# The diagonal of the HGRN2 scores from eight 64-by-64 products instead of four 128-by-128 ones

## The chip, the cores and the metric

The kernel runs on one core of a Trainium2 chip, in one launch. The metric is the device time of one execution in microseconds (us), the median of three runs: 2370.31 us before the change (2369.54 to 2370.97). All numbers by engine come from one profiled execution of the kernel before.

Five engines take part. PE (TensorE) multiplies matrices and writes the results to PSUM; PEld is its weight load. DVE (VectorE) and ACT (ScalarE) do elementwise work and read PSUM. POOL (GpSimd) does elementwise work too. SP (SyncE) issues the transfers (DMA). Each engine works through its own list of instructions in order, and waits where an instruction needs what another engine has not yet finished.

## The reference

Two layers over x of shape [1, 2048, 1024], in float32. Each layer scales and shifts x by a vector made from c, runs mixers over it, projects the result and adds it to x under a layer norm. Layer 0 holds two mixers, an HGRN2 mixer of four heads of 128 channels and an RWKV7 mixer of eight heads of 64; layer 1 is an RG-LRU. The change lies in the HGRN2 mixer, of which this is the core:

```python
log_f = log(lb + (1 - lb) * sigmoid(z));  k = (1 - lb) * sigmoid(-z)
b = cumsum(log_f) within a chunk of 64 steps
# inside a chunk, for t >= s:
s[t, s] = sum_k q[t, k] * k[s, k] * exp(b[t, k] - b[s, k])
o = s @ i + (q * exp(b)) @ S_in            # S_in: the state carried from chunk to chunk
S_out = exp(b_last) * S_in + (k * exp(b_last - b))^T @ i
o = o * rsqrt(mean(o * o) + eps) * norm_g
```

For t = s the decay factor is exp(0) = 1, so the diagonal of the scores is only the sum over k of q[t, k] * k[t, k].

## The kernel before, in words

The 2048 steps are worked through in two halves (superblocks, `sb`) of 1024, and each of these in two blocks (`b`) of 512. Channels lie on the 128 partitions and time on the free axis. For layer 0, `mix0` (L1227) writes PE's order out by hand: a generator of projections (x times the weights; lines L431 to L433, three products for each pair of tiles) is stepped, and between its steps the steps of the other tasks are put in when they come due: `rate_steps`, `b_steps` (RWKV7) and `a_steps` (HGRN2), for four groups `g` and two blocks `b` each. So PE's list interleaves projections with short pieces of both mixers. The order on DVE and ACT is chosen by the scheduler.

`a_steps` (L630) runs 16 times: 4 heads, 2 superblocks, 2 blocks. Here a run of it is called by the time at which its diagonal products start, as "the run at 202". It builds the score matrix of a block in one standing tile `st` [128, 512], four 128-by-128 squares of two chunks each, as `st[s, t]`:

- Six levels of distance h = 32, 16, 8, 4, 2, 1. For a level, `decays` (L656) makes the decay-weighted k and q (L664 to L667 on DVE, an exponential on ACT), and `scores` (L670) multiplies them: PE, line L679, 64-row by 32-column products for each half square. The result in PSUM (`sc`) is copied to `st` under a mask of the level (L694 on DVE, `copy_predicated`; level 32 by ACT, L691).
- The diagonal: four products of 128 by 128 (L711), `kf` (k) against `q`, into a PSUM tile `scd`; then one masked copy of 128x512 (L712) with `dmask`, the identity.
- The products between the two chunks of a square (`s6`, L730), and the state.

`scd` lies in the PSUM buffer with tag "ta", which the neighbouring steps of `a_steps` use as well. Right behind the diagonal, PE's list has, in 12 of the 16 runs, the first half of the RWKV7 score products of the next block (`psc`, L905), then projections, the state products `pn` (L1078, L1087), and the second half of `psc`. The `psc` tiles share the two "tb" buffers: the second half can only start when DVE has read the first half out of them (L912). The two runs for g = 3 of each superblock have no `psc` behind them; in these, and in the state chain of RWKV7 generally, PE's L1087 and DVE's L1090 take turns: each state product needs the state that DVE has just scaled.

Where the two engines meet (L711 and L712 are changed, the rest is not):

```python
pscs = [ps.tile([P, 4, P], F32, name=f"psc_{nm}_{hd}_{c4}", tag="tb", bufs=2) for hd in range(2)]   # L900
nc.vector.tensor_mul(sc[:, hd, c4 * 4 : c4 * 4 + 4], pscs[hd], msk)                                # L912
```

Of the kernel before, what the change touches and what calls it, by code (L numbers as in the profile page):

```python
# [13 lines left out]
F32 = mybir.dt.float32  # L14
# [9 lines left out]
P = 128  # L24
D = 1024
KT = 8
BLK = 512
# [41 lines left out]
def tile_encoder(  # L69
# [19 lines left out]
    nc = tc.nc  # L89
# [28 lines left out]
    ps = ctx.enter_context(tc.tile_pool(name="ps", bufs=1, space=PSUM))  # L118
# [174 lines left out]
    dmask = cst.tile([P, P], U8, name="dmask")  # L293
# [332 lines left out]
    for i in range(1):  # L626
        t = cst.tile([P, BLK], F32, name=f"st_{i}")
        nc.gpsimd.memset(t, 0.0)
        st_tiles.append(t)
    def a_steps(hh, sb, b, us):  # L630

        q, z, iv = (us[i][b][:, 0:BLK] for i in range(3))
        nm = f"a{hh}_{sb}_{b}"

        def t2k(tag, bufs=1, dt=F32):
            return tp.tile([P, BLK], dt, name=f"{tag}_{nm}", tag=tag, bufs=bufs)
# [11 lines left out]
        kf = t2k("a_e")  # L648
# [3 lines left out]
        st = st_tiles[0]  # L652
# [3 lines left out]
        def decays(li):  # L656

            h = LEVELS[li]
            w = tp.tile([P, BLK], F32, name=f"w{li}_{nm}", tag="a_w", bufs=2)
            if h == 1:  # L660
                nc.scalar.activation(w, lf, AF.Exp)
            else:
                mid = half(bb, h)[:, :, 0, h - 1 : h].broadcast_to([P, BLK // (2 * h), h])
                nc.vector.tensor_add(half(w, h)[:, :, 0], half(kz, h)[:, :, 0], mid)  # L664
                nc.vector.tensor_sub(half(w, h)[:, :, 1], half(bb, h)[:, :, 1], mid)
                nc.scalar.activation(w, w, AF.Exp)
            nc.vector.tensor_mul(half(w, h)[:, :, 1], half(w, h)[:, :, 1], half(q, h)[:, :, 1])  # L667
            return kf if h == 1 else w, w

        def scores(lis, ws):  # L670

            sc = ps.tile([P, 2, 4, 32], F32, name=f"sc{lis[0]}_{nm}", tag="oa")
            for i, (li, (left, right)) in enumerate(zip(lis, ws)):
                h = LEVELS[li]
                m = 32 if h == 32 else 64
                for j in range(4):
                    for hf in range(2):
                        o_ = j * P + 64 * hf
                        nc.tensor.matmul(  # L679
                            sc[64 * hf : 64 * hf + m, i, j], left[:, o_ : o_ + m],  # L680
                            half(right[:, o_ : o_ + 64], h)[:, :, 1], start=True, stop=True,
                        )
            for i, li in enumerate(lis):
                h = LEVELS[li]
                m = 32 if h == 32 else 64
                for hf in range(2):
                    rows = slice(64 * hf, 64 * hf + m)
                    stv = st.rearrange("p (j b n two h) -> p j b n two h", j=4, b=2, two=2, h=h)[rows, :, hf, :, 1]
                    scv = sc[rows, i].rearrange("p j (n h) -> p j n h", h=h)
                    if h == 32:  # L690
                        nc.scalar.copy(stv, scv)  # L691
                    else:
                        mask = lmask[rows, li].rearrange("p (j n h) -> p j n h", j=1, h=h)
                        nc.vector.copy_predicated(stv, mask.broadcast_to([m, 4, 32 // h, h]), scv)  # L694
# [10 lines left out]
        ws = decays(1), decays(2)  # L705
        yield 4
        scores((1, 2), ws)
        sc = ps.tile([P, BLK], F32, name=f"scd_{nm}", tag="ta")
        for j in range(4):
            js = slice(j * P, (j + 1) * P)  # L710
            nc.tensor.matmul(sc[:, js], kf[:, js], q[:, js], start=True, stop=True)  # L711
        nc.vector.copy_predicated(  # L712
            st.rearrange("p (j t) -> p j t", j=4), dmask.rearrange("p (j t) -> p j t", j=1).broadcast_to([P, 4, P]),
            sc.rearrange("p (j t) -> p j t", j=4),
        )
        ws = decays(3), decays(4)

        v64 = lambda t: t.rearrange("p (c t) -> p c t", t=64)
# [29 lines left out]
        for j in range(4):  # L748
            js = slice(j * P, (j + 1) * P)
# [20 lines left out]
        for j in range(4):  # L770
            js = slice(j * P, (j + 1) * P)
# [26 lines left out]
    for i in range(2):  # L798
        t = cst.tile([P, 8, 64], F32, name=f"tt_{i}")
# [427 lines left out]
    def mix0(sb, hs, w_first):  # L1227
# [30 lines left out]
        for g in range(4):  # L1258
            for b in range(2):
                early = 4 if g == 3 and b else 0  # L1260
                tasks.append((34 + 48 * g + 24 * b - early, rate_steps(g, sb, b, lr, sgi_of)))
                tasks.append((40 + 48 * g + 24 * b - early, (g, b, b_steps, ub)))
                tasks.append((64 + 48 * g + 24 * b, (g, b, a_steps, ua)))
# [136 lines left out]
```

## Time and profile before

| what | value |
|---|---|
| median of three runs | 2370.31 us (2369.54 to 2370.97) |
| profiled execution, its own time | 2367.25 us, span 2365.5 us |
| PE busy | 2194.7 us, 93% of the span |
| PEld busy | 1727.5 us, 73% |
| DVE busy | 1455.6 us, 62% |
| ACT busy | 1264.6 us, 53% |
| POOL busy | 557.7 us, 24% |
| mean granted clock of PE | 0.969 of full speed |

How to read it: an engine's busy time is the time in which it executes something; the rest is waiting. PE is busy nearly all the time, so a place at which PE waits for another engine is rare, and each can be looked up. The page's table of 40 slices shows that PE's clock (PEclk) is at full speed in most slices. A float32 product shows as two records in the trace, so four products of L711 are eight records. In a timeline, equal instructions behind one another are merged ("x8"), and the idle time before an instruction stands in brackets with what ended it. A start minus the start before it is the pace at which the engine goes through its list; durations of neighbours overlap a little.

### The profile page before, as it was taken

Reading aid. Unit: us, or ns where it says so; the run is one execution under the profiler, and the core shown is the slowest. Engines: PE = TensorE matmul, PEld = TensorE weight load, DVE = VectorE, ACT = ScalarE, POOL = GpSimd, SP = SyncE. Lnnn points to the kernel's source line nnn. Section 1 sums busy time; section 2 is a strip of 40 time slices with the busy share of each in tenths; the row PEclk is TensorE's granted clock in tenths of the full one; section 3 lists DMA queues with packets and bytes.
Section 4 is the critical chain, followed back from the end, with each engine's and each line's share of the span. In section 5 each row is a group of like instructions: output and inputs, shape, how many; then the busy total and the mean of one; then the engine's idle time right before and its main releaser. Section 6 shows DMA issues by size and latency. Waiting matters only on the chain. (4 is left out here: it accounts for less than half of the span.)

```text
span 2365.5 us, 45520 instructions
## 1 busy us (share of the span) xinstructions
PE 2194.7 (93%) x18400; PEld 1727.5 (73%) x18400; DVE 1455.6 (62%) x2697; ACT 1264.6 (53%) x2035; POOL 557.7 (24%) x586
## 2 busy tenths in 40 slices
PE   5989999999999999799999999899999999989998
PEld 4767777777777877577677777678777788767776
DVE  6546666667643678466675666436766556766366
ACT  4344655446666633445565456774467643666541
POOL 3311111212111322112111111112334331353321
PEclk7989999999999999899999999999999999999999
DMA  8210111111332637111111113326311564112652
GB/s 299 92 38 27 40 36 35 44 25 42 97 114 82 223 123 248 35 31 38 33 41 35 44 25 118 112 84 237 130 59 63 169 218 156 63 58 94 200 182 98
DMA packets 185938, 229.82 MB, mean 97 GB/s; under 512 B 65912, under 2 KB 99320, under 8 KB 185728
## 3 DMA queue, kind: packets, MB, share of 16 engines
q1 hardware_dynamic: 185728, 226.92, 30.1%
q8 instruction: 144, 2.36, 0.4%
q14 instruction: 66, 0.54, 0.1%
HBM read 175.46 MB, written 51.39 MB: 96 GB/s over the span
## 5 line engine op out<-in xcount | busy, mean ns | idle before, releaser
L431 PE MATMUL pp_g<-hl_h,wh_g 128*128 128x512 f32 x512 | 212.0, 414 | 4.0 <-ACT go L595 4.0
L433 PE MATMUL pp_g<-hh_h,wl_g 128*128 128x512 f32 x512 | 204.0, 398 | 4.0 <-POOL wl_g L368 4.0
L432 PE MATMUL pp_g<-hh_h,wh_g 128*128 128x512 f32 x512 | 204.4, 399 | 0.0
L368 POOL TENSOR_TENSOR wl_g<-raw_g,wh_g 128x512 fp32r<-128x512 f32 x64 | 97.5, 1528 | 349.9 <-ACT wh_g L367 307.8
L431 PE MATMUL po<-hl_wo,wh_mx 128*128 128x512 f32 x448 | 176.3, 393 | 4.0 <-DVE y L527 4.0
L433 PE MATMUL po<-hh_wo,wl_mx 128*128 128x512 f32 x448 | 175.4, 391 | 0.0
L432 PE MATMUL po<-hh_wo,wh_mx 128*128 128x512 f32 x448 | 174.9, 390 | 0.0
L431 PE MATMUL pp_b<-hl_h,wh_b 128*128 128x512 f32 x384 | 167.8, 437 | 5.1 <-ACT cr_b L838 5.1
L431 PE MATMUL pp_a<-hl_h,wh_a 128*128 128x512 f32 x384 | 168.9, 440 | 0.0
L432 PE MATMUL pp_b<-hh_h,wh_b 128*128 128x512 f32 x384 | 153.5, 400 | 0.0
L432 PE MATMUL pp_a<-hh_h,wh_a 128*128 128x512 f32 x384 | 153.4, 399 | 0.0
L433 PE MATMUL pp_a<-hh_h,wl_a 128*128 128x512 f32 x384 | 153.1, 399 | 0.0
L433 PE MATMUL pp_b<-hh_h,wl_b 128*128 128x512 f32 x384 | 152.7, 398 | 0.0
L368 POOL TENSOR_TENSOR wl_a<-raw_a,wh_a 128x512 fp32r<-128x512 f32 x48 | 66.9, 1402 | 329.0 <-ACT wh_a L367 329.0
L368 POOL TENSOR_TENSOR wl_mx<-raw_mx,wh_mx 128x512 fp32r<-128x512 f32 x64 | 80.8, 1268 | 255.7 <-ACT wh_mx L367 255.7
L368 POOL TENSOR_TENSOR wl_b<-raw_b,wh_b 128x512 fp32r<-128x512 f32 x48 | 67.4, 1409 | 269.1 <-ACT wh_b L367 260.0
L431 PEld LDWEIGHTS pp_g<-hl_h,wh_g 128*128 128x128 f32 x512 | 99.0, 193 | 27.8 <-ACT go L595 4.9
L433 PEld LDWEIGHTS pp_g<-hh_h,wl_g 128*128 128x128 f32 x512 | 99.0, 193 | 27.6 <-POOL wl_g L368 5.7
L587 DVE TENSOR_TENSOR go<-go,oi 128x512 f32<-128x512 f32 x64 | 45.9, 722 | 111.0 <-DMA oi<-o_dr 63.8
L432 PEld LDWEIGHTS pp_g<-hh_h,wh_g 128*128 128x128 f32 x512 | 99.4, 194 | 18.9
L433 PE MATMUL pp_c<-hh_h,wl_c 128*128 128x512 f32 x256 | 101.3, 397 | 11.0 <-POOL wl_c L368 9.6
L431 PE MATMUL pp_c<-hl_h,wh_c 128*128 128x512 f32 x256 | 101.6, 397 | 2.7 <-DVE hl_h L368 2.6
(355 smaller groups left out, 5677.8 us busy)
## 6 DMA issues: line engine op xcount, KB each, us to landing
adw<-in_ada_w_dram SPq DMA_DIRECT2D x96, 256.0 KB
oi<-o_dr SPq DMA_DIRECT2D x64, 256.0 KB
m_dr<-go SPq DMA_DIRECT2D x56, 256.0 KB
raw_b<-in_w_ev_dram SPq DMA_DIRECT2D x48, 256.0 KB
raw_a<-in_w_ev_dram SPq DMA_DIRECT2D x48, 256.0 KB
raw_g<-in_w_ev_dram SPq DMA_DIRECT2D x32, 256.0 KB
wo<-in_w_evo_dram SPq DMA_DIRECT2D x32, 256.0 KB
raw_mx<-m_dr SPq DMA_DIRECT2D x32, 256.0 KB
```

The source lines that it names most:

```text
L368: return (eng or nc.vector).tensor_tensor(out=lo, in0=src, in1=hi.bitcast(F32), op=ALU.subtract)
L431: nc.tensor.matmul(pt, ah, bl, start=first, stop=False)
L432: nc.tensor.matmul(pt, ah, bh, start=False, stop=False)
L433: nc.tensor.matmul(pt, al, bh, start=False, stop=last)
L587: nc.vector.tensor_mul(go[b], go[b], oi[b])
```

## The change

The four 128-by-128 products of the diagonal become eight of 64 by 64, one for each chunk: for `hf` = 0 they write PSUM partitions 0 to 63, for `hf` = 1 partitions 64 to 127, in turn, as the level scores of L679 do. All 128 channels are still summed over. The PSUM tile shrinks to [128, 4, 64]. Since the two halves now lie at other places of `st`, the one masked copy of 128x512 becomes two of 64x256, one for each half.

```diff
-        sc = ps.tile([P, BLK], F32, name=f"scd_{nm}", tag="ta")
+        sc = ps.tile([P, 4, 64], F32, name=f"scd_{nm}", tag="ta")
         for j in range(4):
-            js = slice(j * P, (j + 1) * P)
-            nc.tensor.matmul(sc[:, js], kf[:, js], q[:, js], start=True, stop=True)
-        nc.vector.copy_predicated(
-            st.rearrange("p (j t) -> p j t", j=4), dmask.rearrange("p (j t) -> p j t", j=1).broadcast_to([P, 4, P]),
-            sc.rearrange("p (j t) -> p j t", j=4),
-        )
+            for hf in range(2):
+                o_ = slice(j * P + 64 * hf, j * P + 64 * hf + 64)
+                nc.tensor.matmul(sc[64 * hf : 64 * hf + 64, j], kf[:, o_], q[:, o_], start=True, stop=True)
+        for hf in range(2):
+            rows = slice(64 * hf, 64 * hf + 64)
+            mask = dmask[rows, 64 * hf : 64 * hf + 64].rearrange("p (j t) -> p j t", j=1)
+            nc.vector.copy_predicated(
+                st.rearrange("p (j b t) -> p j b t", b=2, t=64)[rows, :, hf], mask.broadcast_to([64, 4, 64]), sc[rows]
+            )
```

Line numbers behind the diagonal grow by three (L905 becomes L908, L912 L915, L1090 L1093). PE's list is otherwise the same. The scheduler moves a few instructions on DVE.

DVE at the diagonal of the first run, before. L694 copies the level scores, L664 and L665 prepare the next two levels, L667 finishes them:

```order
L694 COPY_PREDICATED st_348<-lmask,sc_a_0_0_1706 64x4x4x8 x2
L664 TENSOR_TENSOR w_a_0_0_1733<-a_kz_a_0_0_1448,a_b_a_0_0_1446 128x64x4
L712 COPY_PREDICATED st_348<-dmask,scd_a_0_0_1727 128x512
L665 TENSOR_TENSOR w_a_0_0_1733<-a_b_a_0_0_1446 128x64x4
L664 TENSOR_TENSOR w_a_0_0_1738<-a_kz_a_0_0_1448,a_b_a_0_0_1446 128x128x2
```

The same place of DVE's list, after:

```order
L694 COPY_PREDICATED st_348<-lmask,sc_a_0_0_1706 64x4x4x8 x2
L716 COPY_PREDICATED st_348<-dmask,scd_a_0_0_1727 64x4x64 x2
L664 TENSOR_TENSOR w_a_0_0_1738<-a_kz_a_0_0_1448,a_b_a_0_0_1446 128x64x4
L665 TENSOR_TENSOR w_a_0_0_1738<-a_b_a_0_0_1446 128x64x4
L664 TENSOR_TENSOR w_a_0_0_1743<-a_kz_a_0_0_1448,a_b_a_0_0_1446 128x128x2
```

The masked copies now stand ahead of the first L664; everything from the second L664 on follows in the same order as before, down to L912. It is the same in the other runs with a `psc` behind them.

DVE at the diagonal of the last run of the first superblock (g = 3, b = 1), before. L1090 scales the state that PE's next L1087 needs; L587 belongs to the output gate:

```order
L664 TENSOR_TENSOR w_a_0_1_7712<-a_kz_a_0_1_7463,a_b_a_0_1_7461 128x128x2
L712 COPY_PREDICATED st_348<-dmask,scd_a_0_1_7701 128x512
L587 TENSOR_TENSOR go_0_4_7537<-go_0_4_7537,oi_1_0_0_7668 128x512
L665 TENSOR_TENSOR w_a_0_1_7712<-a_b_a_0_1_7461 128x128x2
L720 TENSOR_TENSOR a_kz_a_0_1_7463<-a_kz_a_0_1_7463,a_b_a_0_1_7461 128x512
L1090 TENSOR_SCALAR sb_b_0_1_7628<-pn_b_0_1_7629,lam_b_0_1_6516 128x64
L667 TENSOR_TENSOR w_a_0_1_7707<-w_a_0_1_7707,u_a_3_1_6542 128x64x4
```

The same place, after:

```order
L716 COPY_PREDICATED st_348<-dmask,scd_a_0_1_7736 64x4x64 x2
L587 TENSOR_TENSOR go_0_4_7572<-go_0_4_7572,oi_1_0_0_7703 128x512
L664 TENSOR_TENSOR w_a_0_1_7752<-a_kz_a_0_1_7498,a_b_a_0_1_7496 128x128x2
L665 TENSOR_TENSOR w_a_0_1_7752<-a_b_a_0_1_7496 128x128x2
L723 TENSOR_TENSOR a_kz_a_0_1_7498<-a_kz_a_0_1_7498,a_b_a_0_1_7496 128x512
L667 TENSOR_TENSOR w_a_0_1_7747<-w_a_0_1_7747,u_a_3_1_6572 128x64x4
L1093 TENSOR_SCALAR sb_b_0_1_7663<-pn_b_0_1_7664,lam_b_0_1_6546 128x64
```

The state's L1090 (now L1093) has moved behind the first L667.

## Rows read from the trace of the kernel before

**Rows 1.** The page's first part: busy time, share and instructions of each engine.
```profile
PE 2194.7 (93%) x18400; PEld 1727.5 (73%) x18400; DVE 1455.6 (62%) x2697; ACT 1264.6 (53%) x2035; POOL 557.7 (24%) x586
```
**Rows 2.** Timeline of PE, run at 274: start us, us, engine line op.
```profile
272.63 1.13 PE L679 MATMUL sc_a<-w_a 128*64 128x32 f32 x32
273.68 1.16 PE L711 MATMUL scd_a<-u_a,a_e_a 128*128 128x128 f32 x8
274.77 1.16 PE L905 MATMUL psc_b<-zr_b,bk_b 64*128 64x128 f32 x16
...
278.83 1.15 PE L1078 MATMUL pn_b<-sv_b,bkt_b 128*64 128x64 f32 x32
...
280.17 1.40 PE L905 MATMUL psc_b<-zr_b,bk_b 64*128 64x128 f32 x16
```
**Rows 3.** Timeline of PE, 64-by-64 products that all write one half.
```profile
223.38 0.66 PE L730 MATMUL s_a<-u_a,a_kz_a 128*64 128x64 f32 x8
223.97 1.01 PE L944 MATMUL pk_b<-ident,bk_b 64*128 64x64 f32 x16
```
**Rows 4.** Waits: who waited for whom: us in total, times, longest.
```profile
PE psc_b L905 <- DVE zb_b L912: 7.4, 12, 0.8
```
**Rows 5.** Timeline of PE, second half of psc in the run at 202.
```profile
208.94 0.48 PE L905 MATMUL psc_b<-zr_b,bk_b 64*128 64x128 f32 x2 [0.64 <-DVE zb_b L912]
...
210.24 2.02 PE L905 MATMUL psc_b<-zr_b,bk_b 64*128 64x128 f32 x14 [0.81 <-DVE zb_b L912]
```
**Rows 6.** Timeline of DVE, run at 202.
```profile
203.50 1.25 DVE L694 COPY_PREDICATED st<-lmask,sc_a 64x128 f32<-64x128 uint8 x4
204.78 0.43 DVE L664 TENSOR_TENSOR w_a<-a_kz_a,a_b_a 128x256 f32<-128x256 f32 x1
205.22 0.74 DVE L712 COPY_PREDICATED st<-dmask,scd_a 128x512 f32<-128x512 uint8 x1
205.86 0.41 DVE L665 TENSOR_TENSOR w_a<-a_b_a 128x256 f32<-128x256 f32 x1
206.19 0.42 DVE L664 TENSOR_TENSOR w_a<-a_kz_a,a_b_a 128x256 f32<-128x256 f32 x1
206.53 0.41 DVE L665 TENSOR_TENSOR w_a<-a_b_a 128x256 f32<-128x256 f32 x1
...
209.50 0.68 DVE L912 TENSOR_TENSOR zb_b<-psc_b,bmask 128x512 f32<-128x512 f32 x1
```
**Rows 7.** Timeline of DVE, start of the evacuation in the run at 274.
```profile
273.80 1.26 DVE L694 COPY_PREDICATED st<-lmask,sc_a 64x128 f32<-64x128 uint8 x4 [0.30 <-PE sc_a L679]
```
**Rows 8.** Timelines of PE and DVE, run at 716.
```profile
721.57 0.33 PE L1087 MATMUL pn_b<-sb_b,zb_b 64*64 64x64 f32 x4 [0.92 <-DVE sb_b L1090]
...
721.43 0.75 DVE L667 TENSOR_TENSOR w_a<-w_a,u_a 128x256 f32<-128x256 f32 x2
```
**Rows 9.** Timeline of PE, first wait behind the run at 641.
```profile
681.61 0.50 PE L785 MATMUL pss_a<-a_kz_a,ones_r 128*128 128x512 f32 x1 [1.55 <-ACT a_kz_a L780]
```
**Rows 10.** Stretches: length, busy by engine, then PEclk, DMA share, GB/s.
```profile
208.00:210.30 2.30, 0.85 (x16) 0.53 (x10) 2.30 (x6) 0.86 (x2) 0.00 (x0) 1.00 0.05 11
210.30:213.70 3.40, 3.40 (x18) 2.89 (x19) 1.43 (x4) 0.00 (x0) 0.00 (x0) 0.50 0.02 2
...
357.10:360.50 3.40, 3.40 (x26) 2.55 (x23) 1.57 (x3) 0.00 (x0) 0.00 (x0) 1.00 0.07 7
```
**Rows 11.** Timeline of PE, the second half of psc in the run at 349.
```profile
355.42 0.49 PE L905 MATMUL psc_b<-zr_b,bk_b 64*128 64x128 f32 x2 [0.61 <-DVE zb_b L912]
356.67 0.60 PE L905 MATMUL psc_b<-zr_b,bk_b 64*128 64x128 f32 x6 [0.76 <-DVE zb_b L912]
```
**Rows 12.** Timeline of PE, starts of the diagonal in three runs.
```profile
201.99 1.16 PE L711 MATMUL scd_a<-u_a,a_e_a 128*128 128x128 f32 x8
...
348.54 1.16 PE L711 MATMUL scd_a<-u_a,a_e_a 128*128 128x128 f32 x8
...
418.55 1.16 PE L711 MATMUL scd_a<-u_a,a_e_a 128*128 128x128 f32 x8
```

## The prediction

> **What bounds the kernel now.** I read the page's busy table first: PE is busy 93% of the span, DVE 62% [rows 1]. By that alone, work taken from PE is time won. Next the timeline of PE around the diagonal, to see what the four products take and what stands behind them: they run from 273.68 to 274.77, 1.09 us, and the first half of `psc` (L905) follows at once [rows 2]. Then the list of waits, filtered to PE: "psc_b L905 <- DVE zb_b L912" stands there with 7.4 us in 12 cases [rows 4]. They are six of the 16 runs with two waits each: the b = 0 runs of g = 0 to 2 in both superblocks. They lie some 7 us behind the diagonal, before the second half of `psc` [rows 5]. Last the timeline of DVE over that stretch: from the evacuation of the level scores (L694) to the second L912 it has no idle bracket, and from 208.0 to 210.3 it is busy 2.30 of 2.30 us while PE works 0.85 [rows 6, 10].
>
> So the stage with the change has another bound than the kernel as a whole. PE passes the diagonal, does projections, and then stands before buffers that DVE has not yet emptied; DVE is late because L694, L712, L664 to L667 stand ahead of L912 on it. In the six b = 1 runs of g = 0 to 2 the two are level: the second half of `psc` shows no bracket, but takes 1.40 us where the first took 1.16, the sign that its second tile came free late [rows 2]. There too DVE starts at L694, released by PE's level scores (L679), which stand before the diagonal and do not move [rows 7].
>
> **PE.** Removed: 8 records in 1.09 us, start to start. Added: 16 records of 64 by 64, alternating between the two halves of PSUM. The nearest rows are L679, which alternates the same way with 32 columns (32 records in 1.05 us, 0.033 each), and L1078, with 64 (1.15 us for 32, 0.036 each) [rows 2]. Sixteen take 0.53 to 0.58 us, so 0.51 to 0.56 us is saved; I take 0.54. The other end is L730, 64-by-64 products that all write the same half: 8 in 0.59 us, 0.074 each [rows 3]; sixteen would take 1.18 us, a loss of 0.09. I take the former because the new products alternate like L679. On 16 runs PE gets 8.6 us, which is the sum if PE alone were the bound.
>
> **DVE.** Removed: L712, 0.64 us from its start to L665's. It also spread L664 before it to 0.44 us (204.78 to 205.22), where the same form takes 0.34 (206.19 to 206.53) [rows 6]; together 1.08 us. Added: L664 at 0.34 and two masked copies of 64x256. No row shows that size. Below it stands L694 (128 elements a partition), four in 1.28 us, 0.32 each; above it L712 (512), 0.64. By length between them, 256 elements take 0.32 + 0.32/3 = 0.43. So two take 0.85, and the new sequence 1.19: DVE gets to L912 0.11 us later. The bounds: two at 0.32 make 0.10 us earlier, two at 0.64 make 0.54 us later. I take 0.11, because both rows are the same operation and differ in length alone.
>
> **What reaches the end.** In the 12 runs with `psc` behind them PE's 0.54 us only lengthens its wait for L912, and PE goes on 0.11 us later than now: +1.3 us. In the two last runs (g = 3, b = 1), PE's next wait is L1087 for the state that L1090 scales, 0.92 us long [rows 8]. L1090 is now behind the masked copies (+0.11) and behind the first of two L667 that took 0.75 us together (+0.38): +0.49 each, +1.0. In the two g = 3, b = 0 runs PE meets no wait for some 40 us, and the first is local: the sum of squares waits for ACT's square of a product that PE made itself just before [rows 9]. The 0.54 us should stay won: -1.1. Sum +1.2 us. Nothing else is added. In the g = 3 stretches the scheduler swaps a few neighbours: on SP, the transfers of the RWKV inverse (L977, L980) now stand behind one store (L608) and one weight load (L420); the store waits for L587, which DVE now also does just before the inverse's last step, so they are held by an issue at most. On ACT one copy (L935) goes ahead of four exponentials, whose products PE uses only two steps later. I count both as nothing, hidden under the projections in between; if that cover is gone, L994 or L679 would show a wait of some tenths of a microsecond, twice. The smaller PSUM tile uses the same buffer.
>
> **The clock.** The longer waits have a second price. Behind the two waits of the run at 202 (0.64 and 0.81 us) PE's granted clock is 0.50, 1.2 GHz, for 3.4 us; behind those of the run at 349 (0.61 and 0.76) it stays at 1.00, 2.4 GHz [rows 5, 10, 11]. The price can be read: from the diagonal of the run at 202 to the next it takes 273.68 - 201.99 = 71.69 us, from 348.54 to 418.55 70.01 us, the same work: 1.68 us [rows 2, 12]. The six pairs now last 7.4/6 = 1.23 us on average; they will last 1.23 + 0.54 + 0.11 = 1.9 us, and the waits of the last two runs 0.92 + 0.54 + 0.49 = 1.95 us. All eight will be longer than the one pair behind which the clock fell, or as long. The bounds are no further fall at any and a fall at all eight, seven more than now: 0 to 11.8 us. I take three more, +5.0 us: near half, because pairs of 1.37 and 1.45 us went either way, so the length alone does not decide. In the b = 1 runs the new wait (0.54 + 0.11 on top of the 0.24 us within `psc`) is short, and I count no fall.
>
> The Trainium skill's page "TensorE: Matmul & The Clock Gate", section "HAM oscillation — how this bites in real kernels", speaks against this term: it ties the fall to idle gaps that are longer than any of these waits. By that rule nothing more would fall; the trace of the run at 202 does not agree with it. It is the first rival below.
>
> **Sum.** +1.3 + 1.0 - 1.1 + 5.0 = +6.2 us. The durations come from the profiled execution: its own time is 2367.25 us with a span of 2365.5, which would become 2373.5. It lies 3.1 us under the median of the three runs, and I put the sum on the median: 2370.31 + 6.2 = 2376.5 us. What a measurement of this kernel can tell from no change is 0.2%, 4.7 us, so same is 2365.6 to 2375.0.
>
> **Rivals.**
> 1. The clock does not follow: the waits grow, and no more stretches fall (or one). Place: the same eight waits. For it: the run at 349, where 1.37 us of waiting left the clock at full speed. Against it: the run at 202. Time: 2370.31 + 1.2 = 2371.5, to 2373.2 with one fall.
> 2. PE's gain gets through: faster. Mechanism: the second half of `psc` is not held by DVE but only just meets it, so an earlier PE passes. Place: L905 in the six b = 1 runs, which show no bracket today, and the four g = 3 runs. Price: 10 x 0.54 = 5.4 us, 2364.9; if all 16, 2361.7. It decides if L912 ends half a microsecond before PE asks for the buffer. Against it: the 1.40 us of the second half at 280, and a DVE without idle time ahead of it.
> 3. The two short copies cost as much as the long one did: 0.54 us later in 14 places instead of 0.11, 14 x 0.43 = 6.0 us on top: 2382.5. For it: 64 partitions or 128, a copy's time in these rows goes by length, with a large fixed part. Against it: L694 at 0.32.
> 4. The change doesn't do what it says, the eight products not running beside one another (L730's pace). It would cost PE 0.09 us a run, and as PE waits there anyway nothing of that shows in the 12 runs; the waits would hardly grow, the clock would stay, and the time would be 2370.31 + 1.3 + 1.0 + 2 x 0.09 = 2372.8. For it: L730. Against it: L679, just before it, alternates the halves and runs at 0.033.
>
> **How the numbers follow.** The forecast (DVE sets the place, two to five further falls, 2374.8 to 2379.9): 0.49, nearly all slower than 2375.0; I put 0.44 of it to slower and 0.05 to same. Rival 1: 0.25, same. Rival 4, or copies that come out cheaper than reckoned (0.10 us earlier in 14 places, 14 x 0.21 = 2.9 us under rival 1, 2368.6): 0.11, same. Rival 2: 0.09, 0.08 of it faster. Rival 3, or six and more falls: 0.06, slower. So faster 0.08, same 0.42, slower 0.50. The range runs from 2368 (below the cheap copies) to 2383 (rival 3): it leaves out rival 2 and the tail of many falls together with dear copies. The forecast's own range is 2374.8 to 2379.9.
>
> **What would show it.** Right: the diagonal's 16 records take 0.5 to 0.6 us; the masked copies take about 0.45 us each; L905's waits for L912 rise from 7.4 us to 11 or more, and appear in b = 1 runs where there were none; PE's busy time falls while the span does not; more stretches with PEclk 0.50 behind these waits. Wrong: waits for L912 that stay at 7.4 us while the diagonals get nearer to each other; masked copies under 0.35 or over 0.6 us; L1087's waits in the last runs unchanged; distances between diagonals that are the same as now within 0.2 us although the waits are longer, which would leave rival 1.

## The result and the profile after

The changed kernel takes 2380.14 us (median, 2375.46 to 2385.43) where the kernel before, beside it, takes 2370.35: a ratio of 1.0053 [1.0037, 1.0068]. Run again later beside other kernels it took 2379.64 us, 1.0056 [1.0042, 1.0071]. It is slower by half a per cent, in the direction forecast, and 3.1 to 3.6 us above the 2376.5 of the forecast.

The profiled execution took 2385.43 us with a span of 2383.7, which makes it the slowest of its six: its clock shows more of the effect than a typical run. The first part of the page:

```profile
PE 2205.8 (93%) x18528; PEld 1732.2 (73%) x18528; DVE 1459.1 (61%) x2713; ACT 1265.8 (53%) x2035; POOL 559.9 (23%) x586
```
PE's diagonal products take 0.5 us less in each of 16 runs (below), and yet PE is busy 11 us longer than in [rows 1]. Work that shrinks while its time grows is the first sign of the clock.

The timeline of PE in the first run of the diagonal (at 200 here, at 202 before):

```profile
199.82 0.66 PE L679 MATMUL sc_a<-w_a 128*64 128x32 f32 x16 [0.85 <-DVE w_a L667]
200.31 0.66 PE L712 MATMUL scd_a<-u_a,a_e_a 128*64 128x64 f32 x16
200.90 1.16 PE L908 MATMUL psc_b<-zr_b,bk_b 64*128 64x128 f32 x16
...
207.68 0.48 PE L908 MATMUL psc_b<-zr_b,bk_b 64*128 64x128 f32 x2 [1.57 <-DVE zb_b L915]
208.87 1.88 PE L908 MATMUL psc_b<-zr_b,bk_b 64*128 64x128 f32 x14 [0.71 <-DVE zb_b L915]
```
The eight products, 16 records, take 200.90 - 200.31 = 0.59 us where four, 8 records, took 1.09 [rows 2]. All of that, and more, stands again in the bracket before the second half of `psc`: 1.57 and 0.71 us, where it was 0.64 and 0.81 [rows 5]. The 1.88 us of the last group, 14 records where 16 take 1.16 at full speed, is the clock (before, in the one such place, 2.02 [rows 5]).

DVE in the same run:

```profile
201.92 1.26 DVE L694 COPY_PREDICATED st<-lmask,sc_a 64x128 f32<-64x128 uint8 x4
203.22 0.90 DVE L716 COPY_PREDICATED st<-dmask,scd_a 64x256 f32<-64x256 uint8 x2
204.13 0.42 DVE L664 TENSOR_TENSOR w_a<-a_kz_a,a_b_a 128x256 f32<-128x256 f32 x1
...
204.81 0.42 DVE L664 TENSOR_TENSOR w_a<-a_kz_a,a_b_a 128x256 f32<-128x256 f32 x1
...
206.93 0.69 DVE L915 TENSOR_TENSOR zb_b<-psc_b,bmask 128x512 f32<-128x512 f32 x1
207.54 0.68 DVE L728 TENSOR_TENSOR u_a<-u_a,a_b_a 128x512 f32<-128x512 f32 x1
208.14 0.68 DVE L915 TENSOR_TENSOR zb_b<-psc_b,bmask 128x512 f32<-128x512 f32 x1
```
Two more rows of the kernel before, one of PE and one of DVE (the first L912 of its run):

```profile
201.40 0.66 PE L679 MATMUL sc_a<-w_a 128*64 128x32 f32 x16 [0.85 <-DVE w_a L667]
...
208.19 0.69 DVE L912 TENSOR_TENSOR zb_b<-psc_b,bmask 128x512 f32<-128x512 f32 x1
```
In both kernels L694 starts 2.10 us behind PE's L679. Measured from the start of L694: the second L664 comes at 2.89 us instead of 2.69, the first L915 at 5.01 instead of 4.69, the second at 6.22 instead of 6.00 [rows 6]. DVE is 0.2 to 0.3 us later. With that the bracket can be rebuilt. PE would have asked for the buffer at 207.68 - 1.57 = 206.11, 4.19 us behind L694's start; before, at 208.94 - 0.64 = 208.30, 4.80 us behind it. So the first wait grew by 0.61 (PE earlier) + 0.32 (DVE later) = 0.93 us, which is 1.57 - 0.64.

Two groups of the list of waits, us in total, times, longest:

```profile
PE psc_b L908 <- DVE zb_b L915: 16.6, 18, 1.6
...
PE pn_b L1090 <- DVE sb_b L1093: 4.0, 2, 2.0
```
They were 7.4 in 12 [rows 4], and 1.8 in 2, one of them the 0.92 of [rows 8]. Six of the 18 are new, one in each b = 1 run.

Stretches behind four of the eight places with long waits (length, busy by engine, then PEclk, DMA share, GB/s):

```profile
209.10:212.50 3.40, 3.40 (x18) 2.85 (x17) 1.29 (x2) 0.00 (x0) 0.00 (x0) 0.50 0.03 4
...
724.50:727.90 3.40, 3.40 (x15) 2.21 (x11) 1.02 (x4) 0.26 (x1) 0.00 (x0) 0.50 0.00 0
...
1181.90:1185.30 3.40, 3.22 (x17) 2.81 (x18) 1.68 (x5) 0.00 (x0) 0.00 (x0) 0.50 0.00 0
...
1554.00:1557.40 3.40, 3.40 (x15) 2.13 (x11) 1.04 (x4) 0.28 (x1) 0.00 (x0) 0.50 0.00 0
```
PEclk is 0.50 in each, 1.2 instead of 2.4 GHz, and it is the same behind the other four (355.9, 502.7, 1035.1, 1328.7). Before, one of the eight had such a stretch [rows 10]. Two of them last 6.8 us here, the others 3.4: 34 us in all against 3.4, which costs half, some 15 us.

For a typical run the mean granted clock of each execution tells more than one trace: (1 - clock) x span is an estimate of the time lost to the clock; it counts also the time at half clock in which PE waits. It is 71.0 us on average over 17 runs of the kernel before and 84.4 us over the six runs of the changed kernel beside them: 13.4 us more, while the medians differ by 13.2. What is left of the span when that is taken off, the rest, is 2294.1 and 2293.1 us on average. By this estimate all other terms of the change together come to nothing, to within some 2 us by the spread of the runs; the loss is the clock.

### The profile page after: what moved, and what is told of

Same layout as the page of the kernel before. It is cut to its first block, busy times and chain, and to the rows that moved or that the text cites. A ratio compares the mean times of both kernels' runs of the same rounds, so it can differ in the third digit from the quotient of the medians.

```text
span 2383.7 us, 45790 instructions
## 1 busy us (share of the span) xinstructions
PE 2205.8 (93%) x18528; PEld 1732.2 (73%) x18528; DVE 1459.1 (61%) x2713; ACT 1265.8 (53%) x2035; POOL 559.9 (23%) x586
## 5 line engine op out<-in xcount | busy, mean ns | idle before, releaser
L431 PE MATMUL pp_b<-hl_h,wh_b 128*128 128x512 f32 x384 | 172.7, 450 | 8.1 <-ACT cr_b L841 7.5
L368 POOL TENSOR_TENSOR wl_mx<-raw_mx,wh_mx 128x512 fp32r<-128x512 f32 x64 | 80.7, 1266 | 256.5 <-ACT wh_mx L367 256.5
L587 DVE TENSOR_TENSOR go<-go,oi 128x512 f32<-128x512 f32 x64 | 46.1, 722 | 114.8 <-DMA oi<-o_dr 68.3
L431 PEld LDWEIGHTS pp_b<-hl_h,wh_b 128*128 128x128 f32 x384 | 76.9, 200 | 38.7 <-issue 10.6
```

What stands on the lines that cost most here:

```text
L368: return (eng or nc.vector).tensor_tensor(out=lo, in0=src, in1=hi.bitcast(F32), op=ALU.subtract)
L431: nc.tensor.matmul(pt, ah, bl, start=first, stop=False)
L587: nc.vector.tensor_mul(go[b], go[b], oi[b])
```

## The experiments

One table first. "Lost" is (1 - clock) x span, mean of each kernel's runs; "waits" is the group `psc_b` <- `zb_b` (L905 <- L912 before) of the profiled run, us and times; "half" says behind how many of the six pairs of waits, in b = 0 runs, PEclk was 0.50 in that run (in e6, e7, e9 and e10 it is one wait in place of a pair). The edits below are shortened.

| kernel | median us | ratio to before | lost | waits | half |
|---|---|---|---|---|---|
| before | 2366 to 2370 | 1 | 71 to 74 | 7.4, 12 | 1 |
| changed, again | 2379.64 | 1.0056 [1.0042, 1.0071] | 84 | 16.6, 18 | 6 |
| e1: two copies alone | 2380.85 | 1.0057 [1.0038, 1.0076] | 82 | 9.1, 12 | 2 |
| e2: eight products alone | 2367.27 | 0.9999 [0.9986, 1.0012] | 72 | 13.2, 18 | 3 |
| e3: products twice | 2373.76 | 1.0028 [1.0014, 1.0043] | 77 | 10.9, 18 | 2 |
| e4: half by half | 2378.26 | 1.0048 [1.0032, 1.0064] | 83 | 13.1, 18 | 5 |
| e5: copies late | 2352.65 | 0.9927 [0.9905, 0.9949] | 71 | 7.0, 12 | 2 |
| e6: before, copy late | 2362.64 | 0.9972 [0.9956, 0.9989] | 74 | 3.6, 6 | 0 |
| e7: before, more copy | 2365.84 | 0.9983 [0.9967, 0.9999] | 74 | 4.3, 6 | 0 |
| e8: products, one copy late | 2354.49 | 0.9934 [0.9909, 0.9960] | 73 | 7.1, 12 | 1 |
| e9: multiply late | 2369.96 | 1.0017 [1.0004, 1.0031] | 79 | 8.4, 6 | 4 |
| e10: both late | 2349.53 | 0.9945 [0.9925, 0.9965] | 76 | 2.7, 6 | 0 |
| e11: copies twice | 2402.84 | 1.0158 [1.0141, 1.0175] | 96 | 26.7, 24 | 6 |

**e1, the two copies alone.**
```diff
-copy_predicated(st, dmask, sc)                       # 128x512
+for hf in range(2):                                  # 64x256 each, from the four 128x128 products
+    copy_predicated(st[rows, :, hf], mask, sc[rows, :, hf])
```


> The change's part on DVE alone: four 128-by-128 products as before, and the two 64x256 masked copies. Theory (PE stands before buffers that DVE empties; time that PE saves only lengthens its wait, and behind the longer waits its clock falls more often): the pairs of waits of L905 for L912 grow by 0.11 us only, from 1.23 to about 1.35 us, none or up to three places more fall to the half clock, 1.68 us each: 2371.5 to 2376 us, where the changed kernel has 2380.1. Rival (the two copies and the order that comes with them are what costs): 2378 to 2382, as the changed kernel.

It took 2380.85 us: the whole loss of the change, without its products. The rival's number, not mine. PE's part stands as before, and DVE reaches its second L915 (L912) 207.62 - 201.42 = 6.20 us behind L694, as late as in the changed kernel:

```profile
199.32 0.66 PE L679 MATMUL sc_a<-w_a 128*64 128x32 f32 x16 [0.86 <-DVE w_a L667]
199.91 1.16 PE L711 MATMUL scd_a<-u_a,a_e_a 128*128 128x128 f32 x8
201.00 1.16 PE L908 MATMUL psc_b<-zr_b,bk_b 64*128 64x128 f32 x16
...
201.42 1.25 DVE L694 COPY_PREDICATED st<-lmask,sc_a 64x128 f32<-64x128 uint8 x4
...
207.62 0.68 DVE L915 TENSOR_TENSOR zb_b<-psc_b,bmask 128x512 f32<-128x512 f32 x1
```
Beside the same rows of the changed kernel the rows of PE also give PE's full saving: 0.10 us in front of the diagonal (0.59 to 0.49) and 0.50 on it (1.09 to 0.59).

**e2, the eight products alone.**
```diff
 matmul(sc[64*hf : 64*hf+64, j], kf[:, o_], q[:, o_])  # eight, as in the change
-for hf in range(2): copy_predicated(...)              # two of 64x256
+copy_predicated(st, dmask, sc[:, j, None, :])         # one of 128x512, each product read for both halves
```


> The change's part on PE alone: eight 64-by-64 products, and one masked copy over 128x512 that reads each product for both halves of the columns. Theory: the copy stays at 0.65 to 0.75 us, the pairs of waits grow by PE's half microsecond to about 1.75 us, and most of the eight places fall to the half clock: 5 to 7 more at 1.68 us, less 1.1 us won in the two g = 3, b = 0 runs: 2376 to 2381 us. Rival (copies and order cost): the copies are gone, so 2362 to 2370.5 us, from all of PE's gain to none of it.

0.9999: PE's saving alone neither costs nor brings anything. DVE's copy stayed as long as it was, and the second L914 (L912) comes 207.90 - 201.90 = 6.00 us behind L694, as before:

```profile
201.90 1.26 DVE L694 COPY_PREDICATED st<-lmask,sc_a 64x128 f32<-64x128 uint8 x4
...
203.63 0.74 DVE L713 COPY_PREDICATED st<-dmask,scd_a 128x512 f32<-128x512 uint8 x1
...
207.90 0.68 DVE L914 TENSOR_TENSOR zb_b<-psc_b,bmask 128x512 f32<-128x512 f32 x1
```
The waits grew to 13.2 us, 5.8 more than before where the changed kernel has 9.2 more, but half of the six pairs had no half-clock stretch behind them. Both expectations of the theory, here and in e1, were missed.

**e3, the products done twice.**
```diff
-for j in range(4):
+for j in [0, 1, 2, 3] * 2:
```


> The changed kernel with its eight products done twice, one after the other into the same places: 0.5 us more work for PE in each of 16 runs, the DVE work unchanged. Theory: PE is again as late as in the kernel before, the pairs of waits shrink to about 1.35 us, the further falls of the clock go with them, and although it does more it is faster than the changed kernel: 2371.5 to 2376 us against 2380.1. Rival (copies and order cost): 2378 to 2382, no change against the changed kernel. Rival (PE's own work sets the time): 2388, slower by 16 x 0.5 us.

```profile
199.96 1.13 PE L712 MATMUL scd_a<-u_a,a_e_a 128*64 128x64 f32 x32
201.02 1.16 PE L908 MATMUL psc_b<-zr_b,bk_b 64*128 64x128 f32 x16
```
The diagonal is back at 1.06 us, the waits shrink by 5.7 us, and the kernel takes 2373.76, in the range of the theory: by the ratios (1.0028 against 1.0056) half the loss is gone in a kernel that does 128 products more. PE's own work does not set the time here. But e1, with PE as late, kept the whole loss, so this run does not say that PE's earliness is the cause.

**e4, one half of PSUM after the other.**
```diff
-for j in range(4):
-    for hf in range(2):
+for hf in range(2):
+    for j in range(4):
```


> The changed kernel with the eight products in another order: first the four of the lower half of PSUM, then the four of the upper, nothing else. If products beside one another in different halves are what brought 16 records down to 0.44 us, these take the pace of L730, 0.06 to 0.074 us each, 0.95 to 1.2 us together, as long as the four of before; then by the theory of the waits the time goes to 2371.5 to 2376 us. If the order makes no difference to PE, or if the copies are what costs, it stays at 2378 to 2382 us.

```profile
199.77 0.94 PE L712 MATMUL scd_a<-u_a,a_e_a 128*64 128x64 f32 x16
200.64 1.16 PE L908 MATMUL psc_b<-zr_b,bk_b 64*128 64x128 f32 x16
```
0.87 us instead of 0.59 (the 0.44 of the expectation is not what the changed kernel's rows show): alternating between the halves, two records take 0.074 us where two into the same half take 0.109. The saving is down to 0.22 us, and the time stays at 2378.26, the second of the two cases expected.

After these four the theory was turned round: DVE's lateness at L912 costs, not PE's earliness.

**e7, DVE later by 0.3 us, as planned.**
```diff
 copy_predicated(st, dmask, sc)                       # 128x512
+copy_predicated(st[:, :128], dmask, sc[:, :128])
```


> The kernel before (four products, one masked copy), with one more masked copy of 128x128 behind it that copies cells again which the first has just copied: about 0.3 us more on DVE in each of 16 runs, ahead of L912, and nothing else. Theory now, after the first four runs (what PE saves costs and brings nothing; that DVE comes to L912 0.27 us later is what costs, a little as a longer wait, most of it as stretches at half clock behind the longer waits): the pairs of waits grow by 0.3 us, and the time goes to 2376 to 2383 us, as with the two copies alone (2380.9). Rival (it is the form of the two copies, or where L1090 stands behind them, not DVE's lateness): 12 x 0.3 = 3.6 us and no more, 2367 to 2371 us.

A failed dose. The scheduler answered it by putting the second L913 (L912) ahead of the multiply of `u_a`:

```profile
202.49 1.26 DVE L694 COPY_PREDICATED st<-lmask,sc_a 64x128 f32<-64x128 uint8 x4
...
207.62 1.29 DVE L913 TENSOR_TENSOR zb_b<-psc_b,bmask 128x512 f32<-128x512 f32 x2
208.81 0.69 DVE L726 TENSOR_TENSOR u_a<-u_a,a_b_a 128x512 f32<-128x512 f32 x1
```
DVE does more and is done with the second L913 earlier; waits fall to 4.3 us, and the kernel is 0.17% faster than before. It tells nothing of a late DVE, but it does tell that more work on DVE need not cost.

**e5, e6, e8: the copies moved behind L912.** In e5 (two copies, eight products), e6 (one copy, four products) and e8 (one copy, eight products) the copy stands two steps further down in the code:
```diff
-for hf in range(2): copy_predicated(st[...], mask, sc[rows])
 ws = decays(3), decays(4)
 ...
 yield 6
+for hf in range(2): copy_predicated(st[...], mask, sc[rows])
 scores((3, 4), ws)
```


> The changed kernel with its two masked copies moved on DVE from ahead of L664 to ahead of the scores of the next levels, behind the L912s that PE waits for; nothing left out. Theory (DVE's lateness at L912 costs): DVE comes to L912 0.9 us earlier than in the changed kernel and 0.65 us earlier than before; the pairs of waits go from about 2.3 to 1.4 us or less, fewer stretches at half clock, and PE's half microsecond begins to count: 2355 to 2366 us. Rival (the copies cost wherever they stand): 2376 to 2382 us.

> The kernel before with its one masked copy moved to the same place; four products. Theory: DVE comes to L912 about 0.65 us earlier, PE meets it nearly without a wait, pairs of waits under 0.6 us: 2352 to 2362 us. Rival (DVE's place does not matter): 2363 to 2369 us, as before.

> Eight products, one masked copy over 128x512 that reads each product for both halves of the columns, and that copy moved to the same later place. Theory: DVE is as early at L912 as in the kernel before with its copy moved, and PE comes half a microsecond earlier: waits of about 1.2 us a pair are left. Between the changed kernel with its copies moved and the kernel before with its copy moved, 2352 to 2364 us; if PE's gain gets through once DVE is out of the way, 4 to 8 us under the latter.

DVE in e5:
```profile
203.41 1.24 DVE L694 COPY_PREDICATED st<-lmask,sc_a 64x128 f32<-64x128 uint8 x4
204.66 0.42 DVE L664 TENSOR_TENSOR w_a<-a_kz_a,a_b_a 128x256 f32<-128x256 f32 x1
...
208.67 0.69 DVE L916 TENSOR_TENSOR zb_b<-psc_b,bmask 128x512 f32<-128x512 f32 x1
...
209.46 0.91 DVE L728 COPY_PREDICATED st<-dmask,scd_a 64x256 f32<-64x256 uint8 x2
```
The second L916 (L912) comes 5.26 us behind L694 instead of 6.22, and the copies run where PE hardly waits for them (0.7 us in two cases). The same work in another place takes 2352.65 us, 27 less than the changed kernel and 0.73% less than before. Against the changed kernel about half of that is the clock (84 to 71 us lost); against the kernel before most of it is not: the rest falls from 2292 to 2281 us there, the lost time only from 74 to 71. e6 is 0.28% faster than before. Between e6 and e8 the copies stand alike and the products differ: 2362.64 to 2354.49, 8.2 us, or 0.51 for each of 16 runs. That is PE's saving, most of the 0.60 us shown by e1, arriving once DVE is not in the way; by the spread of the runs the 8.2 us may be anything from 3 to 11. (e6 came in at the upper end of what I expected, just past it by 0.6 us.)

**e9, the second L912 ahead of the multiply; e10, that and the copies late.**
```diff
-nc.vector.tensor_mul(qe, q, eb)
 yield 6
+nc.vector.tensor_mul(qe, q, eb)
```


> The changed kernel with one multiply of DVE (u_a by a_b_a, 0.6 us, between the two L912s of a pair) moved behind the second L912; products and both copies stay as they are. Theory (what counts is when DVE reaches the second L912): it comes 0.6 us earlier, the pairs of waits go from about 2.3 to 1.7 us, and the time to 2362 to 2371 us, the kernel before or a little less. Rival (the two copies cost by their form, or by where L1090 stands in the g = 3 runs): 2376 to 2382 us as the changed kernel.

> Both moves together: the changed kernel with its two copies behind the L912s, and the multiply behind the second L912. Theory: DVE reaches the second L912 1.5 us earlier than in the changed kernel; of the 7.0 us of waits that were left with the copies moved, 12 of 0.6, nearly none is left, and the time goes 2 to 8 us under that kernel's 2352.7: 2344 to 2351 us. If waits below half a microsecond cost nothing any more: 2351 to 2354 us.

PE in e9, then in e10:
```profile
207.03 1.75 PE L908 MATMUL psc_b<-zr_b,bk_b 64*128 64x128 f32 x16 [1.58 <-DVE zb_b L915]
```
```profile
206.07 1.75 PE L909 MATMUL psc_b<-zr_b,bk_b 64*128 64x128 f32 x16 [0.64 <-DVE zb_b L916]
```
In e9 products and copies are those of the change, and of its excess 70% is gone (1.0017 against 1.0056) because one wait of 1.58 us stands in place of 1.57 + 0.71. In e10 the wait is 0.64, and through the whole passage the clock stays up, in this run and behind all six waits:
```profile
203.00:216.00 13.00, 12.25 (x120) 8.57 (x120) 8.80 (x20) 5.55 (x10) 0.00 (x0) 1.00 0.06 8
```
2349.53 us is the lowest median of all; by the intervals e10 and e5 can't be told apart, so that the second move adds something is not shown. Nor is e10 faster than the kernel before by the clock: its six executions lose 76 us to it on average, where the kernel before beside it loses 71, and the rest falls from 2294 to 2274 us. Where e10 loses its clock instead is not shown.

**e11, DVE later by 0.9 us.**
```diff
 for hf in range(2): copy_predicated(st[...], mask, sc[rows])
+for hf in range(2): copy_predicated(st[...], mask, sc[rows])
```


> The changed kernel with its two masked copies done twice, one pair right behind the other: 0.9 us more for DVE in each of 16 runs, PE's work and the order of the rest as they are in the 12 runs with psc behind them. Theory (DVE's lateness at L912 sets the place of PE): 12 x 0.9 = 10.8 us as longer waits, 1 to 2 us in the g = 3 runs, and none to eight more stretches at half clock: 2391 to 2406 us. Rival (PE has slack there, and the copies cost by their form alone): 2380 to 2384 us.

```profile
208.54 0.79 PE L914 MATMUL psc_b<-zr_b,bk_b 64*128 64x128 f32 x2 [2.48 <-DVE zb_b L921]
209.74 2.07 PE L914 MATMUL psc_b<-zr_b,bk_b 64*128 64x128 f32 x14 [0.41 <-DVE zb_b L921]
```
```profile
283.30:286.70 3.40, 3.40 (x12) 2.21 (x12) 1.18 (x3) 0.00 (x0) 0.00 (x0) 0.50 0.12 12
358.40:365.20 6.80, 6.24 (x26) 4.72 (x27) 2.34 (x6) 0.00 (x0) 0.00 (x0) 0.50 0.08 10
```
Here the order kept, and the dose took: 2402.84 us, 23 more than the changed kernel beside it. The waits grew by 26.7 - 16.6 = 10.1 us (12 x 0.9 = 10.8 were reckoned), and 12 us more are lost to the clock. Half-clock stretches now stand behind b = 1 runs too (283.3).

**e12, the changed kernel again.**

> The changed kernel as it is, beside the three on the same chip: 2376 to 2383 us, and in its trace, as in the first, half-clock stretches behind most of the eight places with long waits (six pairs of L908, two L1090). If fewer than five of the eight show one, the first trace was not typical of it.

```profile
208.50:211.90 3.40, 3.20 (x17) 2.79 (x18) 1.70 (x5) 0.00 (x0) 0.00 (x0) 0.50 0.00 0
...
722.90:726.30 3.40, 3.40 (x21) 2.22 (x20) 0.92 (x4) 0.56 (x1) 0.00 (x0) 1.00 0.00 0
...
1550.00:1553.40 3.40, 3.40 (x13) 2.24 (x12) 1.02 (x4) 0.17 (x1) 0.00 (x0) 0.50 0.00 0
```
Seven of the eight places, all but the one at 722.9. The first trace was typical in that.

**What stays open.** e1 loses as much to the clock as the whole change (82 us) with waits that are only 1.7 us longer in total than before, and in its trace two of six pairs fell. That trace is of its fastest run, 2373.20 us; where the slower ones lost their clock no trace shows. That later DVE makes longer waits and longer waits more stretches at half clock is shown by e5, e9 and e11, each against the changed kernel; that this is all of what happens in e1 is not. The length of these waits does not put the first three experiments in order: e2 and e3 have more of it than e1 (13.2 and 10.9 us against 9.1) and lose less to the clock (72 and 77 against 82).

## Why the prediction was right, and where not

- **The bound.** Right. The second half of `psc` waits for DVE; what PE saves before it stands in the wait behind. e2 (nothing won) and e6 against e8 (8.2 us won with DVE out of the way) show both sides. Rival 2, PE's gain getting through, falls: in the kernel as it was, it doesn't. The Trainium skill's page "TensorEngine Tiling (Array Packing)", section "PSUM Bottleneck", says of products made small to lie side by side that they speed up TensorE but not the emptying of PSUM, which may become the bottleneck once TensorE is four times as fast. The traces agree in kind: the eight products take 0.59 us instead of 1.09, not yet twice as fast, the emptying 0.90 instead of 0.74, and DVE was what PE waited for before the change already.
- **PE's term.** Taken as 0.54 us; 0.50 on the diagonal and 0.10 ahead of it. Rival 4 falls: alternating between the halves, the products take 0.59 us, and e4 shows what they take when they don't alternate, 0.87 us.
- **DVE's term.** The copies were taken at 0.43 and take 0.444 on average, so rival 3 falls. The sum was still too small: 0.11 us taken, 0.20 at the second L664 and 0.22 at the second L912. From the first copy's start to L664's it is 0.91 us, where the sum had 0.85; the rest are a few hundredths in the neighbours.
- **The last runs, and the gain kept.** L1090's waits were taken as 1.95 us and are 2.0. In the two g = 3, b = 0 runs 0.54 us each were to stay won; with the same time lost to the clock, the way to the next diagonal is 718.19 - 643.28 = 74.91 us instead of 716.24 - 641.03 = 75.21, and 75.19 instead of 75.38 in the other, so about half did.
- **The clock.** The places were right, the number was not: three more stretches taken, seven and six more found in the two traces, two of them of double length in the first and one in the second. This is the mis-sized term: +5.0 us stood in the sum, and 13.4 us are measured. Six and more falls had been given 0.06, together with rival 3. Rival 1, no further falls, is wrong. The Trainium skill's page "TensorE: Matmul & The Clock Gate" has also a section, "A second HAM failure mode: psum-queue depth-cycling", on another kernel in which short idle times between groups of products, often enough, make the clock swing. The traces agree with that one: 1.57 and 0.71 us, and 0.50 behind them.
- **The step that failed** is the reason given for the clock's term: that PE's saved half microsecond makes the waits long enough. It lengthens them, but alone it costs nothing (e2), while the 0.2 to 0.3 us by which the copies delay DVE bring the whole loss alone (e1). I had counted DVE's part as a small shift of 0.11 us and looked for the falls on PE's side.

The direction was right in part by luck: it hung on the clock's term, which was put down to a saving that alone costs nothing, and three falls were a choice between none and seven. The net came out near because the other terms, +1.2 us together in the forecast and -1.0 (2293.1 - 2294.1) by the runs, are small in both, and because the clock's term, though less than half of what is measured, had the right sign.

## What to carry to other kernels

Before an engine is made faster, find which engine's instruction ends the next wait on its path, and count the change in that engine's queue up to that instruction: a fifth of a microsecond there decided, half a microsecond on the busier engine did not. Where a waiting PE has its clock cut, as it was here behind all twelve of the changed kernel's pairs, a wait is charged twice, so work that nobody waits for soon (here the masked copies) belongs behind the instruction that PE waits for; that move alone turned +0.5% into -0.7%. And where a scheduler orders the queue, look at the order it made: an added instruction can bring another one forward (e7).

## What the runs showed of the hardware

- Half-clock stretches stand more often behind longer waits. Over the 14 traces, with the one or two waits of L905 for L912 in a run of the diagonal taken together, a stretch at 0.50 began within some 4 us behind none of 57 that came to less than 1.1 us, 7 of 17 from 1.25 to 1.5, 14 of 21 from 1.5 to 1.75, 8 of 11 from 1.75 to 2.0, and all 14 above that. The length alone does not decide: of e9's six single waits the longest, 1.58 us, kept the full clock, and one of 1.25 us did not.
- Runs of the kernel before spread by 14 to 18 us within a round, and the time lost to the clock goes with the span: one run took 2360.00 us at a mean clock of 0.972 and one 2375.01 at 0.966. By (1 - clock) x span they differ by 80.7 - 66.0 = 14.7 of the 15.0 us. That is a clear case; over all 68 runs the correlation of the two is 0.85.
- The records of fp32 products of 64 by 64 that alternate between the halves of PSUM come every 0.59/16 = 0.037 us, those into one half every 0.87/16 = 0.054 us.
- A masked copy took 0.30 us for 128 elements a partition, 0.44 for 256 on 64 partitions and 0.74 for 512 on 128.
